# A two-layer encoder trunk on one core: seven-product tiles woven with plain tiles, and five groups of hidden values turned by VectorE

## The chip, the core and the metric

The kernel runs on one NeuronCore of one Trainium2 chip. A core has five engines that run their own instruction streams and wait for each other through semaphores: TensorE (PE; matrix products, into eight PSUM banks), VectorE (DVE), ScalarE (ACT), GpSimd (POOL) and SyncE (SP, which here only issues DMA transfers). The metric is the device time of one execution in microseconds (us); for the kernel before it is 938.8 us, the median of three runs (938.33 to 939.52).

## The reference

256 tokens of width 1024 go through two layers. A layer is a half-step SwiGLU feed-forward block, a mixing block (a windowed attention and a differential attention side by side) and a second feed-forward block. The change lies in the feed-forward blocks alone, of which there are four, called FFN 1 to FFN 4 here:

```python
D_MODEL, SEQ, DEPTH, D_FF = 1024, 256, 2, 2816

def swiglu(h, w_gate, w_up, w_down):
    return (jax.nn.silu(h @ w_gate) * (h @ w_up)) @ w_down

for l in range(DEPTH):
    x = x + 0.5 * swiglu(rms_norm(x, ffn1_norm[l]), ffn1_w_gate[l], ffn1_w_up[l], ffn1_w_down[l])
    ...
    x = x + 0.5 * swiglu(rms_norm(x, ffn2_norm[l]), ffn2_w_gate[l], ffn2_w_up[l], ffn2_w_down[l])
return rms_norm(x, final_norm)
```

All is float32.

## The kernel before

**Weight tiles.** A feed-forward block reads its weights in tiles of 512 rows by 512 columns (1 MB), in an order fixed in a list (`specs`, filled in `ffn_specs`, L244 to L261). A tile is loaded into one of six `raw` buffers by a DMA that SP issues (`emit_dma`, L148). Then it is split for the float32 product into a high part, rounded by ScalarE (a cast), and a remainder, subtracted by VectorE (`emit_split`, L176), in two halves of two row blocks each. The split halves lie in 14 `w` buffers, so seven halves, three and a half tiles, can stand ready. A product of two split operands takes three matmuls (high by high, remainder by high, high by remainder).

`weights()` (L233) is called where TensorE's instructions for the next tile are written. It first emits the splits that lie six halves ahead and the loads that fit into the raw buffers (`ahead`, L212), and the second half of a tile is emitted ahead in the same way when TensorE's instructions reach it. During the feed-forward blocks TensorE, VectorE, ScalarE and GpSimd execute their instructions in the order in which the program writes them (`Kept`, L41); each waits at its own instruction until what it needs is there. SP's DMAs are ordered by the scheduler of the framework, and executed in that order.

**Groups.** The 2816 hidden columns are five groups of 512 and a last one of 256. For a *plain* group, `tokens` (L496) multiplies the 256 tokens (two row blocks) by two gate tiles and two up tiles, 24 matmuls a tile, each into two PSUM banks; `gate` and `hidden` form Silu(gate) times up (ScalarE, then one VectorE "up" operation per row block).

Groups 2 and 4 (`SEVEN`) are done by seven products instead of eight. Tokens in two halves and input columns in two halves make four quarters of the operand; the tile's gate and up rows in two halves make four weight blocks: a (gate, first rows), b (up, first rows), c (up, last rows), d (gate, last rows). The seven products, 12 matmuls each (`prod`, L590), use sums and differences of the quarters (made once per block by `make_sums`, L333) and the weights a, b + c, d, c, a + b, a + b + c and a + b + c + d. Two of the sums, b into a and c into b, are made by DMAs that GpSimd issues and that add onto the raw buffer; the other two by VectorE, in pairs of adds on raw buffers. `by_seven` (L600) issues the products one after the other, with one of the two down tiles of the group before after the fourth and the other at the end, and combines them with seven VectorE operations of 128x512 and two "up" operations.

**Turning.** The hidden values have tokens on partitions, and the down product needs hidden columns there. Two ways are in the kernel. `turn` (L636) does it on TensorE: 8 transposes of 128x128 into two banks, then split by ScalarE and VectorE from PSUM. A `Flip` (L648) does it without TensorE: VectorE transposes 32x32 blocks, one instruction for each of the two row blocks; then eight DMAs of 64 KB, issued by SP, carry the block rows to their partitions; and `operands` (L658) lets ScalarE and VectorE split the result from SBUF. Before, `made` (L670) uses a Flip for groups 0 and 2 (`FLIP`), except in FFN 1, where `aside` is `attention_constants`. So groups 0 to 4 of FFN 1 and groups 1, 3 and 4 of the other three blocks are turned on TensorE: 14 turns. The last group of 256 columns is always turned there.

**Order of a block.** Group n's first tile, the turn of group n - 1, the rest of group n, then the two down tiles of group n - 1 (`down`, L678), which add into four PSUM banks kept through the block (L676). Four banks are left for everything else. After the last group's two tiles, `ffn_end` (L730) multiplies by group 4's down tiles. In FFN 1 and FFN 4 an `aside` is emitted ahead of group 3: the constants for attention (one TensorE transpose, VectorE and ScalarE operations), and the load of the final gain.

Of the kernel before, what the change touches and what calls it, by code (L numbers as in the profile page):

```python
# [18 lines left out]
FF = 2816  # L19
# [12 lines left out]
FLIP = (0, 2)  # L32
# [3 lines left out]
def trunk(ctx: ExitStack, tc: tile.TileContext, x, n1, g1, u1, d1, nm, w_in, sink,  # L36
# [79 lines left out]
    def seven(wg, wu, c0, downs):  # L116

        a, b, c, d = [object() for _ in range(4)]  # L120
        w = {a: rows(wg, c0, 512, 0, 4), b: rows(wu, c0, 512, 0, 4), c: rows(wu, c0, 512, 4, 4), d: rows(wg, c0, 512, 4, 4)}

        def load(k):
            return lambda t: [(t, w[k])]

        def gather(k, to):
            def add():
                pool.dma_start(raws[to], w[k], accum_op=ALU.add)
            return add

        def plus(x, to):
            def prep():
                for h in (0, 2):
                    x_, t_ = [raws[i][:, h:h + 2] for i in (x, to)]
                    dve.tensor_tensor(t_, t_, x_, op=ALU.add)
            return prep

        return [Step(4, 512, load(a), key=a, free=[]),
                Step(4, 512, load(b), key=b, behind=gather(c, b), prep=gather(b, a)),
                Step(4, 512, load(d), key=d, free=[]),  # L140
                Step(4, 512, load(c), key=c, free=[]),
                downs[0],
                Step(4, 512, None, src=a, free=[]),
                Step(4, 512, None, prep=plus(c, a), src=a, free=[c]),
                Step(4, 512, None, prep=plus(d, a), src=a, free=[a, d]),
                downs[1]]

# [95 lines left out]
    for l in range(DEPTH):  # L243
        def ffn_specs(wg, wu, wd):  # L244
            down = lambda g, h: plain(wd[l], h * 512, 512, 4 * g, 4)
            for k0 in (0, 4):
                specs.extend(plain(w[l], 0, 512, k0, 4) for w in (wg, wu))
            for g in range(1, NGRP):
                downs = [down(g - 1, h) for h in range(2)]
                if g in SEVEN:  # L250
                    specs.extend(seven(wg[l], wu[l], g * 512, downs))
                else:
                    specs.extend(plain(w[l], g * 512, 512, k0, 4) for w in (wg, wu) for k0 in (0, 4))
                    specs.extend(downs)
            for k0 in (0, 4):
                def gu_moves(t, k0=k0, ws=(wg[l], wu[l])):
                    return [(t[:, :, h * 256:h * 256 + 256], rows(w, FF - 256, 256, k0, 4)) for h, w in enumerate(ws)]
                specs.append(Step(4, 512, gu_moves))
# [31 lines left out]
    class Norm:  # L290
# [42 lines left out]
        def make_sums(self):  # L333
# [5 lines left out]
            def make(x, y, op):  # L339
                v = tmp().rearrange("p a (c s) -> p (a c) s", c=2)  # L340
                dve.tensor_tensor(v, x, y, op=op)
# [9 lines left out]
            s2 = make(s1, t0, ALU.add)  # L351
            yield
            make(t1, t0, ALU.subtract)
            yield
            make(b0, s2, ALU.subtract)
# [212 lines left out]
    def ffn(norm, aside=None, before=None, final=False):  # L568
# [21 lines left out]
        def prod(xo, w):  # L590
            acc = bank()
            for k in range(4):
                hi, lo = w.part(k)
                xh, xl = xo(k)
                pe.matmul(acc, lhsT=xh, rhs=hi, start=k == 0, stop=False)
                pe.matmul(acc, lhsT=xl, rhs=hi, start=False, stop=False)
                pe.matmul(acc, lhsT=xh, rhs=lo, start=False, stop=k == 3)
            return acc

        def by_seven(h, g):  # L600


            flat = lambda: tmp().rearrange("p a n -> p (a n)")

            def put(o, x, y, op):
                dve.tensor_tensor(o, x, y, op=op)
                return o

            m1, m7 = flat(), flat()
            act.copy(m1, prod(norm.quarter(0, 0), weights()))  # L610
            hT = turned(h)
            act.copy(m7, prod(norm.summed(2), weights(held=True)))
            p2 = prod(norm.quarter(0, 1), weights())
            g0 = put(flat(), p2, m1, ALU.add)
            p3 = prod(norm.summed(3), weights())
            silu(g0, g0, 0)
            down(hT, g - 1, 0, weights())
            h = blk(F32)
            p5 = prod(norm.summed(0), weights())
            p6 = prod(norm.summed(1), weights())  # L620
            u2 = put(flat(), p6, m1, ALU.subtract)
            u3 = put(m7, m7, u2, ALU.add)
            p4 = prod(norm.quarter(1, 1), weights())
            g1 = put(m1, p4, u3, ALU.subtract)
            w = weights()
            silu(g1, g1, 1)
            put(u3, u3, p5, ALU.subtract)
            put(u2, u2, p5, ALU.subtract)
            put(u2, u2, p3, ALU.add)
            up(h, u2, g0, 0)  # L630
            up(h, u3, g1, 1)
            h = made(h, g)
            down(hT, g - 1, 1, w)
            return h
# [61 lines left out]
        h = made(hidden(g, us), 0)  # L696
        for n in range(1, NGRP):
            sums = norm.make_sums() if n + 1 == min(SEVEN, default=0) else iter(())
            if n == 3 and aside is not None:
                aside()  # L700
            if n in SEVEN:
                h = by_seven(h, n)
                continue
            gs = [bank(), bank()]
            tokens(gs, norm.xs, weights(), 0)
            hT = turned(h)
            tokens(gs, norm.xs, weights(), 4)
            g = gate(gs)
            next(sums, None)
            us = [bank(), bank()]  # L710
            for k0 in (0, 4):
                tokens(us, norm.xs, weights(), k0)
                next(sums, None)
            h = made(hidden(g, us), n)
            for hh in range(2):
                down(hT, n - 1, hh, weights())
                if hh == 0:
                    next(sums, None)

        gu = [bank(), bank()]  # L720
        tokens(gu, norm.xs, weights(), 0)
        hT = turned(h)
        tokens(gu, norm.xs, weights(), 4)
# [362 lines left out]
```

## Time and profile before

| | |
|---|---|
| median of three runs | 938.8 us |
| profiled execution | 938.07 us |
| its span, first to last instruction | 936.3 us |
| TensorE busy | 924.3 us |
| VectorE busy | 710.7 us |
| ScalarE busy | 551.6 us |
| DMA moved | 189.34 MB, mean 202 GB/s |

The profile is one execution. The span is what the engine times are shares of; the time of a run holds some 2 us more than the span. "PE" is TensorE, "DVE" VectorE, "ACT" ScalarE, "SPq" SyncE's issue of DMAs. In a row of operations the text "out<-in" gives the program's names of the tiles: `ps` is a PSUM bank, `w` a split weight, `raw` a loaded tile, `s` a block of activations or hidden values (also a Flip's), `tmp` an intermediate of 128x512, `ident` the identity of a transpose. `s<-s` is a Flip's transpose, its DMA, or the split behind it. "x24" is a count, and "[0.53 <-DVE s L51]" says that the engine had been idle for 0.53 us and what ended it. All engine instructions are issued through one helper and carry its line, L51, so rows are told apart by tiles.

### The profile page before, as it was taken

The numbers are of one execution on the slowest core, as the hardware profiler recorded it, in microseconds if no ns is written. First come the engines' busy times: TensorE is split into PE (matmuls) and PEld (weight loads), VectorE is DVE, ScalarE is ACT, GpSimd is POOL, SyncE is SP. The second block draws the span as 40 slices with busy tenths as digits, with TensorE's granted clock in tenths as the row PEclk, the third lists the DMA queues.
The fourth block names the chain that finished last, engine by engine and source line by source line (L and its number), as shares of the span: only waits on it lengthen the run. The fifth ranks groups of instructions, "written<-read, shape, count | busy, mean of one in ns | idle before, by whom it ended". The sixth has DMA issues, their size and how long they took to land.

```text
span 936.3 us, 12889 instructions
## 1 busy us (share of the span) xinstructions
PE 924.3 (99%) x4796; PEld 784.7 (84%) x4796; DVE 710.7 (76%) x1010; ACT 551.6 (59%) x869; POOL 41.5 (4%) x65
## 2 busy tenths in 40 slices
PE   8999999999999999999999999999999999999997
PEld 6788788899898888888888888888999888888886
DVE  6679869779856479689765896896796655895992
ACT  7856556467735467276473664565685483664562
POOL 0400000000000000000000001000000000000001
PEclk9999999999999999999999999999999999999999
DMA  9986958746424876978658588686642447588721
GB/s 339 346 225 210 289 131 289 208 176 153 136 75 135 248 199 204 261 211 310 197 178 232 151 302 240 188 299 181 185 147 90 135 163 215 150 303 238 213 91 45
DMA packets 113583, 189.34 MB, mean 202 GB/s; under 512 B 4207, under 2 KB 38065, under 8 KB 113521
## 3 DMA queue, kind: packets, MB, share of 16 engines
q1 hardware_dynamic: 103728, 170.42, 55.0%
q0 software_dynamic: 8704, 17.07, 10.7%
q10 hardware_dynamic: 1088, 1.05, 0.3%
q8 instruction: 37, 0.61, 0.3%
q14 instruction: 26, 0.20, 0.1%
HBM read 184.32 MB, written 1.05 MB: 198 GB/s over the span
## 4 chain that ended last, share of the span: by engine, by line
PE 94%; DVE 2%; ACT 1%; issue 1%; DMA 0%; POOLq 0%; ACTq 0%; POOL 0%; DVEq 0%
PE ps L51 94%; DVE w L51 1%; ACT w L51 1%; DMA xk<-in_x_dram 0%; DVE raw L51 0%; ACT s L51 0%; DVE tmp L51 0%; DVE s L51 0%; ACT tmp L51 0%; ACT L51 0%; DVE xk L51 0%; POOLq L1081 0%; ACTq L51 0%; POOL rf L51 0%; DVE rf L51 0%
## 5 line engine op out<-in xcount | busy, mean ns | idle before, releaser
L51 PE MATMUL ps<-w,s 128*128 128x512 f32 (+1 forms) x2994 | 690.4, 390 | 0.5 <-DVE tmp L51 0.5
L51 PEld LDWEIGHTS ps<-w,s 128*128 128x128 f32 x2994 | 557.4, 188 | 115.8 <-DVE tmp L51 1.5
L51 DVE TENSOR_TENSOR w<-raw,w 128x1024 fp32r<-128x1024 f32 (+1 forms) x416 | 435.0, 1087 | 87.9 <-ACT w L51 85.5
L51 ACT CAST w<-raw 128x1024 fp32r<-128x1024 f32 (+1 forms) x416 | 372.5, 943 | 150.8 <-PE ps L51 93.1
L51 PE MATMUL ps<-s,w 128*128 128x256 f32 x672 | 84.0, 285 | 0.0
L51 PEld LDWEIGHTS ps<-s,w 128*128 128x128 f32 x672 | 81.7, 192 | 1.1
L51 PE MATMUL ps<-w,q 128*128 128x512 f32 x288 | 68.7, 392 | 0.0
L51 PEld LDWEIGHTS ps<-w,q 128*128 128x128 f32 x288 | 53.5, 188 | 10.8
L51 ACT CAST s<-s 128x512 fp32r<-128x512 f32 x12 | 6.9, 619 | 69.6 <-DMA s<-s 55.1
L51 DVE TENSOR_TENSOR s<-s,s 128x512 fp32r<-128x512 f32 x12 | 7.8, 689 | 50.5 <-ACT s L51 50.5
L51 ACT ACTIVATE s<-ps,gcol 128x256 fp32r<-128x256 f32 (+1 forms) x80 | 31.3, 476 | 20.9 <-PE ps L51 20.9
L51 DVE TENSOR_TENSOR raw<-raw,raw 128x1024 f32<-128x1024 f32 x32 | 37.6, 1218 | 0.0
L51 POOL DMA_DIRECT2D raw<-in_ffn_w_up_dram x16 | 20.8, 1298 | 363.6 <-DVE w L51 156.8
L51 ACT ACTIVATE s<-s,negm 128x256 f32<-128x256 f32 x64 | 31.9, 500 | 6.6 <-DVE negm L51 6.6
L51 PE MATMUL ps<-ident,s 128*128 128x128 f32 x256 | 33.6, 273 | 0.8 <-DVE s L51 0.8
L51 PEld LDWEIGHTS ps<-ident,s 128*128 128x128 f32 x256 | 29.5, 141 | 5.1 <-ACT w L51 0.9
L51 ACT CAST s<-ps 128x512 fp32r<-128x512 f32 x36 | 19.6, 591 | 21.9 <-PE ps L51 21.9
L51 DVE TENSOR_TENSOR s<-ps,s 128x512 fp32r<-128x512 f32 x36 | 23.3, 685 | 10.8 <-ACT s L51 10.8
L51 DVE SCALAR_TENSOR_TENSOR s<-ps,gcol,s 128x256 fp32r<-128x256 f32 x48 | 20.3, 478 | 14.6 <-ACT s L51 14.5
L51 ACT ACTIVATE tmp<-tmp,r 128x512 f32<-128x512 f32 x16 | 11.6, 722 | 27.1 <-DVE tmp L51 27.1
L51 ACT CAST q<-tmp 128x512 fp32r<-128x512 f32 x20 | 12.4, 620 | 20.9 <-DVE tmp L51 20.9
L51 ACT ACTIVATE tmp<-ps,r 128x512 f32<-128x512 f32 (+1 forms) x32 | 19.1, 629 | 6.9 <-PE ps L51 6.8
(110 smaller groups left out, 456.5 us busy)
## 6 DMA issues: line engine op xcount, KB each, us to landing
raw<-in_ffn_w_down_dram SPq DMA_DIRECT2D x44, 1024.0 KB, 5.3
raw<-in_ffn_w_gate_dram SPq DMA_DIRECT2D x39, 1024.0 KB, 5.9
raw<-in_ffn_w_up_dram SPq DMA_DIRECT2D x39, 1024.0 KB, 5.2
raw<-in_ffn_w_up_dram POOLq DMA_DIRECT2D x16, 1024.0 KB, 9.7
raw<-in_w_in_dram SPq DMA_DIRECT2D x14, 1024.0 KB, 5.9
raw<-in_ffn_w_gate_dram SPq DMA_DIRECT2D x8, 512.0 KB, 4.5
raw<-in_ffn_w_up_dram SPq DMA_DIRECT2D x8, 512.0 KB, 5.5
raw<-in_w_in_dram SPq DMA_DIRECT2D x8, 512.0 KB, 5.1
```

The lines of the kernel that those rows point to most:

```text
L51: ins = issue(*a, **k)
```

## The change

The order of a feed-forward block, from group 1 on, is written out in one list (`ORDER`), from which both the loads and the instructions are made. Tiles of the seven-groups alternate with tiles of plain groups, down tiles and tiles of the last group. In the terms above, after group 0 the order of tiles is: plain 1, seven 2 a, plain 1, seven 2 d, two of plain 1, seven 2 c, down 0, seven 2 a+b, down 0, seven 2 a+b+c, plain 3, seven 2 b+c, plain 3, seven 2 a+b+c+d, two of plain 3, seven 4 a, down 1, seven 4 d, down 1, seven 4 c, down 2, seven 4 a+b, down 2, seven 4 a+b+c, last, seven 4 b+c, down 3, seven 4 a+b+c+d, last, down 3. Then come group 4's down tiles, as before.

Four of the seven products (a, a+b+c, b+c, a+b+c+d) add one after the other into one PSUM bank, which is read between them; one of the token sums changes its sign for it. The combining takes four VectorE operations and one more ScalarE operation than before. The weights a, d and c of a seven-group stay in their raw buffers until their sums are made.

Groups 0 to 4 are all turned by a Flip, in all four blocks; `turn` remains for the last 256 columns. The `aside` moves behind the last group's second tile, ahead of the second down tile of group 3. The sums of the operand are made from the start of group 1 on.

```diff
-FLIP = (0, 2)
+def order():
+    two, four = [[("seven", g, p) for p in ("a", "d", "c", "ab", "abc", "bc", "abcd")] for g in (2, 4)]
+    one, three = [[("plain", g, (w, k0)) for w in range(2) for k0 in (0, 4)] for g in (1, 3)]
+    downs = [[("down", g, h) for h in range(2)] for g in range(4)]
+    last = [("last", 0, k0) for k0 in (0, 4)]
+    sums = [("sums", 0, 1)]
+    turn = [[("turned", g, 0)] for g in range(4)]
+    aside = [("aside", 0, 0)]
...
+    seq = sums + one[:1] + sums + two[:1] + sums + one[1:2] + sums + two[1:2] + turn[0] + one[2:]
+    seq += two[2:3] + downs[0][:1] + two[3:4] + downs[0][1:]
+    seq += weave(two[4:], three) + turn[1]
+    seq += four[:1] + downs[1][:1] + four[1:2] + turn[2] + downs[1][1:] + four[2:3] + downs[2][:1] + four[3:4] + turn[3] + downs[2][1:] + four[4:5]
+    seq += last[:1] + four[5:6] + downs[3][:1] + four[6:] + last[1:] + aside + downs[3][1:]
+    return seq
...
+        def step(self, part):
+            k = self.key
+            return dict(
+                a=lambda: Step(4, 512, self.load("a"), key=k["a"], free=[]),
+                d=lambda: Step(4, 512, self.load("d"), key=k["d"], free=[]),
+                c=lambda: Step(4, 512, self.load("c"), key=k["c"], free=[]),
+                ab=lambda: Step(4, 512, None, src=k["a"], free=[]),
+                abc=lambda: Step(4, 512, None, prep=self.plus("c", "a"), src=k["a"], free=[k["c"]]),
+                bc=lambda: Step(4, 512, self.load("b"), key=k["b"], behind=self.gather("c", "b")),
+                abcd=lambda: Step(4, 512, None, prep=self.plus("d", "a"), src=k["a"], free=[k["a"], k["d"]]))[part]()
...
+        class Seven:
...
+            def a(self):
+                self.acc = prod(norm.quarter(0, 0))
+                self.m1 = self.flat()
+                act.copy(self.m1, self.acc)
+
+            def d(self):
+                g0 = self.put(prod(norm.quarter(0, 1)), self.m1, ALU.add, self.m1)
+                self.m1 = None
+                self.g0 = silu(g0, g0, 0)
+
+            def c(self):
+                self.z = self.flat()
+                act.copy(self.z, prod(norm.summed(3)))
+
+            def ab(self):
+                p5 = prod(norm.summed(0))
+                self.v = self.flat()
+                act.mul(self.v, p5, -1.0)
+                self.put(self.z, p5, ALU.subtract, self.z)
+
+            def abc(self):
+                prod(norm.summed(1), self.acc)
+                self.put(self.z, self.acc, ALU.subtract, self.z)
+                self.h = blk(F32)
+                up(self.h, self.z, self.g0, 0)
+                self.z = self.g0 = None
+
+            def bc(self):
+                prod(norm.summed(2), self.acc)
+                self.put(self.v, self.acc, ALU.subtract, self.v)
+
+            def abcd(self):
+                prod(norm.quarter(1, 1), self.acc)
+                g1 = silu(self.flat(), self.acc, 1)
+                up(self.h, self.v, g1, 1)
+                self.v = self.acc = None
+                hid[self.g] = Flip(self.h)
...
-        def made(h, g):
-            return Flip(h) if g in FLIP and aside is not attention_constants else h
-
-        def turned(h):
-            return h.operands() if isinstance(h, Flip) else turn(h, 2)
...
+        hid, hT, groups = {0: Flip(hidden(g, us))}, {}, {}
+        sums = norm.make_sums()
+        for what, n, part in ORDER:
...
+            elif what == "down":
+                down(hT[n], n, part, weights())
+                if part:
+                    del hT[n]
+            elif what == "turned":
+                hT[n] = hid.pop(n).operands()
...
+            elif what == "aside" and aside is not None:
                 aside()
...
-        hT = turned(h)
-        tokens(gu, norm.xs, weights(), 4)
+        hT = hid.pop(NGRP - 1).operands()
         h = hidden(gate([b[:, 0:256] for b in gu]), [b[:, 256:512] for b in gu])
         return accs, hT, lambda: turn(h, 1)
```

More of the change, by code (lines that the diff above doesn't have):

```diff
@@ L612, in by_seven @@
[L612 to L622, printed above, removed]
@@ L695, in ffn @@
         tokens(us, norm.xs, weights(), 4)
[L696 to L699, printed above, removed]
-                aside()
[L701 to L722, printed above, removed]
-        tokens(gu, norm.xs, weights(), 4)
+        hid, hT, groups = {0: Flip(hidden(g, us))}, {}, {}
+        sums = norm.make_sums()
+        for what, n, part in ORDER:
+            if what == "seven":
+                getattr(groups.setdefault(n, Seven(n)), part)()
+            elif what == "plain":
+                groups.setdefault(n, Plain(n)).part(*part)
+            elif what == "down":
+                down(hT[n], n, part, weights())
[3 more added lines that the diff above has]
+                hT[n] = hid.pop(n).operands()
+            elif what == "sums":
+                for _ in range(part):
+                    next(sums, None)
+            elif what == "aside" and aside is not None:
+                aside()
+            elif what == "last":
+                if part == 0:
+                    gu = [bank(), bank()]
+                tokens(gu, norm.xs, weights(), part)
+        hT = hid.pop(NGRP - 1).operands()
         h = hidden(gate([b[:, 0:256] for b in gu]), [b[:, 256:512] for b in gu])
```

121 lines of the change are left out of this document (66 added, 55 removed).

## The prediction, made before the result was known

> **What bounds the kernel now.** I read the engine shares first, then the chain that ended last, then a table of one undisturbed stretch (the second feed-forward block, FFN 2), then TensorE's timeline around a turn.
>
> The page's busy shares, and its chain by engine:
>
> ```profile
> PE 924.3 (99%) x4796; PEld 784.7 (84%) x4796; DVE 710.7 (76%) x1010; ACT 551.6 (59%) x869; POOL 41.5 (4%) x65
> ...
> PE 94%; DVE 2%; ACT 1%; issue 1%; DMA 0%; POOLq 0%; ACTq 0%; POOL 0%; DVEq 0%
> ```
>
> The table by stretch (start:end, length, then busy time and instructions of each engine, granted clock, DMA share, GB/s):
>
> ```profile
> 305.00:480.00 175.00, 175.00 (x795) 145.11 (x794) 135.17 (x148) 99.49 (x129) 5.86 (x5) 1.00 0.75 228
> ```
>
> TensorE is busy for all of these 175 us at full clock, while VectorE (third figure) has 40 us to spare and ScalarE 75. So inside a block an instruction taken off TensorE shortens the program by its whole length, and work put on VectorE, ScalarE or a queue costs nothing until TensorE waits for it.
>
> TensorE's timeline in FFN 1: three stretches with a turn in each:
>
> ```profile
> 29.67 6.28 PE L51 MATMUL ps<-w,s 128*128 128x512 f32 x27
> 36.48 0.30 PE L51 MATMUL ps<-ident,s 128*128 128x128 f32 x1 [0.53 <-DVE s L51]
> 37.05 0.98 PE L51 MATMUL ps<-ident,s 128*128 128x128 f32 x7 [0.26 <-DVE s L51]
> 37.79 30.19 PE L51 MATMUL ps<-w,s 128*128 128x512 f32 x132
> 67.81 1.03 PE L51 MATMUL ps<-ident,s 128*128 128x128 f32 x8
> 68.61 2.99 PE L51 MATMUL ps<-w,q 128*128 128x512 f32 x12
> ...
> 94.78 1.29 PE L51 MATMUL ps<-w,s 128*128 128x512 f32 x5
> 96.01 0.25 PE L51 MATMUL ps<-ident,grow 34*128 34x34 f32 x1
> 96.18 0.96 PE L51 MATMUL ps<-w,s 128*128 128x512 f32 x3
> 97.65 5.06 PE L51 MATMUL ps<-w,s 128*128 128x512 f32 x21 [0.50 <-DVE tmp L51]
> ```
>
> Matmuls overlap, so starts are compared, not durations. 132 matmuls from 37.79 to 67.81 are 0.227 us each; a tile of 24 is therefore 5.45 us, a product of 12 is 2.73. A turn, 8 transposes, is 68.61 - 67.81 = 0.80 us. The first turn costs more: 27 matmuls from 29.67 end at 35.80, and the next matmul starts at 37.79, so 1.99 us, as VectorE is late with the hidden values.
>
> **The change part by part.**
>
> *Turns off TensorE.* Turned on TensorE before: groups 0 to 4 in FFN 1, and 1, 3, 4 in FFN 2 to 4, 14 in all; none afterwards. 13 x 0.80 + 1.99 = 12.4 us off the path. This is the whole gain; matmuls are neither added nor removed.
>
> *What VectorE and ScalarE get.* Rows by group and shape (count | busy us, mean ns):
>
> ```profile
> L51 DVE TENSOR_TENSOR w<-raw,w 128x1024 fp32r<-128x1024 f32 x312 | 367.9, 1221 | 71.6 <-ACT w L51 69.6
> L51 ACT CAST w<-raw 128x1024 fp32r<-128x1024 f32 x312 | 313.6, 1052 | 120.3 <-PE ps L51 71.6 <-DVE raw L51 42.2 <-DMA raw<-in_ffn_w_up_dram 2.8
> L51 DVE TENSOR_TENSOR tmp<-ps,tmp 128x512 f32<-128x512 f32 x24 | 16.4, 683 | 0.0
> L51 DVE STREAM_TRANSPOSE s<-s 128x512 f32<-128x512 f32 x12 | 12.3, 1060 | 0.0
> L51 DVE SCALAR_TENSOR_TENSOR s<-ps,hr,tmp 128x512 f32<-128x512 f32 x24 | 16.9, 745 | 0.0
> L51 ACT ACTIVATE tmp<-ps,r 128x512 f32<-128x512 f32 x24 | 15.2, 681 | 1.4 <-PE ps L51 1.4
> L51 DVE TENSOR_TENSOR s<-s,s 128x512 fp32r<-128x512 f32 x12 | 7.8, 689 | 50.5 <-ACT s L51 50.5
> L51 ACT CAST s<-s 128x512 fp32r<-128x512 f32 x12 | 6.9, 619 | 69.6 <-DMA s<-s 55.1 <-DMA s<-in_final_norm_dram 14.5
> L51 ACT COPY tmp<-ps 128x512 f32<-128x512 f32 x16 | 9.4, 586 | 8.2 <-PE ps L51 8.2
> ```
>
> 14 Flips of two transposes at 12.3/12 = 1.03 us are +28.7 us of VectorE. Seven combining adds become four in each of 8 seven-groups: 24 x 0.68 = -16.4 us. The splits behind a turn keep their count. ScalarE gets one evacuation more per seven-group, 8 x 0.59 = 4.7. VectorE comes to about 723 of 930 us, 78%: hidden.
>
> *The weave.* It matters where VectorE's work is dense. A split weight tile is two halves, 2 x 367.9/312 = 2.36 us; a pair of raw adds is about as long. In the old run of a seven-group VectorE has 9 tiles (21.2), two pairs (4.7), seven adds (4.8), two "up" and a Flip (3.6): 34 us against 7 x 2.73 + 2 x 5.45 = 30.0 of TensorE. In the new order the densest run, from the third part of group 2 to its fifth (5 tiles, TensorE 19.1 us), has 11.8 of splits, 4.7 of pairs, 2.1 for two adds and an "up", 3.4 of group 1's "up" and Flip: 22 us, 3 us late. The split runs 3 tiles ahead, at least 2.73 + 5.45 + 2.73 = 10.9 us, so TensorE does not see it. Cost 0; if the lead is gone, 3 us in each block. Nothing here can be gained in FFN 2, whose TensorE is already full.
>
> *One bank for four products.* The product that adds onto the bank must wait for VectorE's read of the sum before. Between them always lies a tile of 24 matmuls, 5.45 us, against 0.68 us of reading and a VectorE up to 3 us late: 0. A plain group beside it finds two of the eight banks fewer, and its "up" half must wait until the gate banks are read: two Silu at 0.68 us against one product, 2.73: 0, with about 1 us to spare.
>
> *The Flip's queue work.* Each Flip issues 8 DMAs on SP. The first two of FFN 2, with what POOL issued beside them and when ScalarE got the data:
>
> ```profile
> 316.83 8.57 SPq L656 DMA_DIRECT2D s<-s  x8
> 384.02 3.14 SPq L656 DMA_DIRECT2D s<-s  x5
> 384.02 8.10 SPq L656 DMA_DIRECT2D s<-s  x8
> ...
> 315.57 1.32 POOL L51 DMA_DIRECT2D raw<-in_ffn_w_up_dram  x1 [9.21 <-DVE s L51]
> 385.18 1.28 POOL L51 DMA_DIRECT2D raw<-in_ffn_w_up_dram  x1 [41.86 <-DVE s L51]
> ...
> 328.05 1.15 ACT L51 CAST s<-s 128x512 fp32r<-128x512 f32 x2 [9.86 <-DMA s<-s]
> 395.87 1.14 ACT L51 CAST s<-s 128x512 fp32r<-128x512 f32 x2 [13.77 <-DMA s<-s]
> ```
>
> First issue to first use is 11.2 and 11.9 us, and both ran into an adding load of POOL. Before that load bites, five issues take 3.14 us, 0.63 each. 112 more DMAs hold SP for up to 14 x 8.6 = 120 us, and the weight loads behind them wait up to 8.6 us each time. Six raw buffers and three split tiles lie ahead of TensorE; where three raw buffers are pinned by a seven-group, three are left, with about 11 us between a buffer's release and the use of its next load. Cost 0, with little to spare.
>
> Groups 0 to 3 have 16.4, more than 30, 21.8 and 27.3 us of other TensorE work between their last matmul and their turn: hidden. **Group 4 has two tiles, 48 x 0.227 = 10.9 us**, and nothing follows them on TensorE but its own down product. Its path after the last matmul: 0.2 to ScalarE (that matmul's tail), Silu 0.68, "up" 0.75, first transpose 1.03, which makes 2.7; eight issues at 0.63, 5.0; from the last issue to ScalarE 328.05 - 325.40 = 2.65; cast 0.62, subtraction 0.69 and 0.1 of handing over. Sum 11.8, needed at 10.9 + 0.23 (the second matmul reads the remainder): 0.7 us of stall. No POOL load is due there, as group 4's second one follows a load issued some 20 us earlier, so I take the quick issue. Bounds: 0, and with issues as slow as 8.57 and a landing of 3.75 us (395.87 - 392.12) 5.4 us. For FFN 2 to 4: 3 x 0.7 = 2.1.
>
> In FFN 1 the attention constants are emitted into exactly that gap:
>
> ```profile
> 100.81 0.19 DVE L51 COPY gcol<-ps 128x34 f32<-128x34 f32 x1
> 103.17 0.41 DVE L51 TENSOR_REDUCE lsum<-s 128x4 f32<-128x256 f32 x1
> 103.61 0.20 ACT L51 ACTIVATE lex<-lsum 128x4 f32<-128x4 f32 x1 [5.34 <-DVE lsum L51]
> ```
>
> These six VectorE operations take 2.8 us and ScalarE waits for their end. Counted from the start of the second-last tile: VectorE is through the Flip and two splits at 6.2, through the constants at 9.0; ScalarE then does the exponential, the two casts that stand behind it (to 11.5) and the turned values; VectorE its five small operations and two splits, to 13.9, then the remainder, to 14.6. Needed at 11.1: 3.5 us. Where the constants stand now TensorE loses 1.0 (94.78 to 97.65 for 8 matmuls of 1.82), which goes.
>
> *Sum.* -12.4 - 1.0 + 3.5 + 2.1 = -7.8 us. Against the profiled run (938.07, span 936.3) 930.3; the median of the three runs is 0.7 higher, so **931**.
>
> The Trainium skill speaks against the edit: "VectorE: DVE Perf Modes", section "The three transpose paths", advises TensorE for a 128x128 transpose whose result may lie in PSUM, at 390 ns. By that figure 112 transposes would free 44 us, an estimate; the trace has 0.10 us each in a row, and it decides. [...]
>
> **The rivals.**
>
> *A, slower: group 4's Flip is as late as today's Flips.* Then all four blocks stall for 5 us: -13.4 + 20 = +7, 946. For it: every measured Flip took 11 to 12 us. Against: each had a POOL load beside it. It turns slower once the stall exceeds 3.4 us a block. A stall this long may also slow the clock: at the program's start 20 matmuls took 6.17 us,
>
> ```profile
> 6.19 6.17 PE L51 MATMUL ps<-w,s 128*128 128x512 f32 x20
> ```
>
> where 4.7 is normal, so 1.5 us more per stall, 952. (The Trainium skill, "TensorE: Matmul & The Clock Gate", part 1, states that an idle window of about 3.4 us halves the clock; the page shows full clock up to its last slice, so no run here shows it yet.)
>
> *B, the weave is late.* Three pinned raw buffers, a bank read late, or SP behind its Flips stall TensorE about 1 us per seven-group: 8 us, 939, no change. For it: VectorE is 3 us late at one place. Against: the old order is denser and FFN 2 shows no idle TensorE.
>
> *C, all hidden.* Group 4's Flip and the constants cost nothing: -13.4, 925.
>
> **How the numbers follow.** Forecast 0.60 (its own range 927 to 935), A 0.17, B 0.13, C 0.10. Low is 925, C's time; high 944, which cuts off most of A: about 0.15 left out above and 0.04 below. A change within 0.2% (1.9 us) cannot be told from none here. Faster: forecast, C and a little of B, 0.72; same 0.06; slower 0.22.
>
> **What would show it.** TensorE's busy time falls by about 12 us and its transposes by 112. In FFN 2, 3 and 4 TensorE idles about 0.7 us just before the first matmul of group 4's down product, ended by VectorE's subtraction; in FFN 1 about 3.5. The Flips of group 4 take 5 to 6 us to issue, those beside POOL's loads 8 or more. Elsewhere in the blocks TensorE does not idle. It is wrong if idle time comes in the woven tiles (B), or if the last Flip's issue takes 8 us (A).

## The result, and the profile after

The changed kernel takes 944.1 us (median of five runs, 941.13 to 946.82) against 938.5 for the kernel before: ratio 1.0058, 95% interval 1.0033 to 1.0083. It is slower by 0.6%; the forecast was 931 and faster. The profiled execution is the shortest of the five: 941.13 us, span 939.4, that is 3.1 us over the profiled execution of before.

From the page of the changed kernel, its engine shares, the chain by engine and two groups of TensorE (busy us, mean ns | idle before, releaser). The helper's line is L77 now, the Flip's DMAs are L728, the weight loads L180:

```profile
PE 916.9 (98%) x4684; PEld 774.1 (82%) x4684; DVE 725.5 (77%) x1014; ACT 564.2 (60%) x877; POOL 42.6 (5%) x65
...
PE 85%; DVE 6%; issue 3%; DMA 2%; ACT 2%; SPq 0%; ACTq 0%; DVEq 0%; POOLq 0%; POOL 0%
...
L77 PE MATMUL ps<-w,s 128*128 128x512 f32 (+1 forms) x2994 | 692.8, 390 | 3.9 <-DVE s L77 3.1
...
L77 PE MATMUL ps<-w,q 128*128 128x512 f32 x288 | 71.2, 397 | 7.7 <-DVE tmp L77 7.7
```

The 112 transposes are gone, but TensorE's part of the chain falls from 94% to 85%. The group `ps<-w,q` now has 7.7 us of idle time ended by VectorE's `tmp`: TensorE waits for the shared bank to be read. `ps<-w,s` has 3.1 us ended by VectorE's `s`: turned hidden values come late.

**The bank.** TensorE, then VectorE, ScalarE, SP and GpSimd in FFN 2 around product b+c of group 2 (timeline: start, us, engine; in brackets the idle time before):

```profile
362.25 2.88 PE L77 MATMUL ps<-w,q 128*128 128x512 f32 x12
364.96 5.60 PE L77 MATMUL ps<-w,s 128*128 128x512 f32 x24
371.34 3.00 PE L77 MATMUL ps<-w,q 128*128 128x512 f32 x12 [0.77 <-DVE tmp L77]
...
360.80 0.68 DVE L77 TENSOR_TENSOR tmp<-tmp,ps 128x512 f32<-128x512 f32 x1
362.89 2.36 DVE L77 TENSOR_TENSOR w<-raw,w 128x1024 fp32r<-128x1024 f32 x2 [1.41 <-ACT w L77]
365.96 2.36 DVE L77 TENSOR_TENSOR w<-raw,w 128x1024 fp32r<-128x1024 f32 x2 [0.71 <-ACT w L77]
368.24 2.35 DVE L77 TENSOR_TENSOR raw<-raw,raw 128x1024 f32<-128x1024 f32 x2
370.51 0.68 DVE L77 TENSOR_TENSOR tmp<-tmp,ps 128x512 f32<-128x512 f32 x1
...
361.80 2.01 ACT L77 CAST w<-raw 128x1024 fp32r<-128x1024 f32 x2 [2.06 <-DMA raw<-in_ffn_w_up_dram]
364.88 2.00 ACT L77 CAST w<-raw 128x1024 fp32r<-128x1024 f32 x2 [1.07 <-DMA raw<-in_ffn_w_gate_dram]
...
350.77 7.61 SPq L728 DMA_DIRECT2D s<-s  x8
358.48 1.28 SPq L180 DMA_DIRECT2D raw<-in_ffn_w_gate_dram  x1
...
352.30 1.28 POOL L77 DMA_DIRECT2D raw<-in_ffn_w_up_dram  x1 [36.52 <-DVE s L77]
```

Product a+b+c (362.25) is done at 365.1. VectorE reads its bank at 370.51, 5.4 us later, because the read stands in VectorE's queue behind a split and the pair of raw adds for a later tile, 4.7 us of work whose results are not yet needed, and behind two waits for ScalarE (1.41 and 0.71). ScalarE in turn waited for the adding load (issued 352.30, used 361.80) and for a gate tile whose load SP issued only after the Flip's eight DMAs (358.48). Product b+c is ready at 370.4 and starts at 371.34: 0.93 us, counted from start to start less 0.227. In FFN 3 and FFN 4 the same wait is 1.24 and 1.28 us. In FFN 1 it is 4.90, TensorE's rows and VectorE's:

```profile
78.47 5.60 PE L77 MATMUL ps<-w,s 128*128 128x512 f32 x24
88.81 4.57 PE L77 MATMUL ps<-w,q 128*128 128x512 f32 x12 [4.74 <-DVE tmp L77]
...
87.98 0.68 DVE L77 TENSOR_TENSOR tmp<-tmp,ps 128x512 f32<-128x512 f32 x1
```

It is the same queue, some 4 us later against TensorE than in FFN 2. VectorE brings that lateness from the start of the block. Its "up" operations of group 0 in FFN 1 and in FFN 2:

```profile
36.06 1.40 DVE L77 SCALAR_TENSOR_TENSOR s<-ps,hr,tmp 128x512 f32<-128x512 f32 x2
...
318.66 1.40 DVE L77 SCALAR_TENSOR_TENSOR s<-ps,hr,tmp 128x512 f32<-128x512 f32 x2
```

TensorE's last matmul of group 0 is over at about 31.0 us in FFN 1 and at 318.65 in FFN 2 (72 matmuls of 0.227 us from 14.64 and from 302.29). So VectorE is at once there in FFN 2 and 5 us late in FFN 1, and it does not catch up before the bank.

The twelve matmuls behind the wait take 4.4 us from start to start instead of 2.73. The stretches say why, and give FFN 2 to its last two tiles (granted clock is the third figure from the end):

```profile
83.00:89.00 6.00, 1.26 (x6) 0.78 (x5) 5.53 (x6) 3.21 (x4) 0.00 (x0) 0.98 1.05 387
89.00:92.00 3.00, 3.00 (x8) 2.32 (x9) 3.00 (x4) 1.80 (x3) 0.00 (x0) 0.50 1.05 388
305.00:460.00 155.00, 153.33 (x673) 125.78 (x672) 127.40 (x131) 94.89 (x114) 5.86 (x5) 1.00 0.81 243
```

The clock is halved after the wait, which costs 1.7 us more (4.40 - 2.73). FFN 2, without an idle moment before, now has 1.7 us.

**Group 1's turn.** FFN 2 before down 1, TensorE, then VectorE:

```profile
389.82 6.51 PE L77 MATMUL ps<-w,s 128*128 128x512 f32 x28
396.80 7.57 PE L77 MATMUL ps<-w,s 128*128 128x512 f32 x32 [0.47 <-DVE s L77]
...
392.74 1.43 DVE L77 SCALAR_TENSOR_TENSOR s<-ps,hr,tmp 128x512 f32<-128x512 f32 x2
394.09 2.08 DVE L77 STREAM_TRANSPOSE s<-s 128x512 f32<-128x512 f32 x2
396.09 1.25 DVE L77 TENSOR_TENSOR s<-s,s 128x512 fp32r<-128x512 f32 x2
```

Group 1's turned values had long arrived. Their subtraction (396.09) stands behind group 3's "up" and transposes, which wait for group 3's last matmul; one product later TensorE needs them. 0.63 us in each of the four blocks.

**Group 4's turn.** FFN 2: SP, ScalarE and TensorE; then TensorE in FFN 1:

```profile
448.43 5.94 SPq L728 DMA_DIRECT2D s<-s  x8
...
456.25 1.14 ACT L77 CAST s<-s 128x512 fp32r<-128x512 f32 x2 [1.39 <-DMA s<-s]
...
456.92 0.50 PE L77 MATMUL ps<-w,s 128*128 128x512 f32 x1 [0.20 <-ACT s L77]
457.65 3.70 PE L77 MATMUL ps<-w,s 128*128 128x512 f32 x15 [0.23 <-DVE s L77]
...
177.56 4.17 PE L77 MATMUL ps<-w,s 128*128 128x512 f32 x17 [1.04 <-DVE s L77]
```

0.86 us in FFN 2, none in FFN 3 and 4, 1.3 in FFN 1.

**The sum, start to start, for the two profiled runs.** Turns off TensorE -12.4, the constants' old wait -1.0; waits for the bank 4.90 + 0.93 + 1.24 + 1.28 = +8.4 and the half clock +1.7; group 1's turn 4 x 0.63 = +2.5; before down 0 of FFN 1 (61 us) +0.9, of which 0.2 is group 0's turned values and 0.7 a split weight behind them in VectorE's queue; group 4's turn 1.3 + 0.86 = +2.2; the program's start, where nothing was changed, +0.7 (the matmuls behind the first 24 begin at 14.64 us instead of 13.91). Together +3.0 against 3.1 measured. The median is 3 us above this profiled run. The five runs' mean granted clocks are 0.996 (941.1 and 942.8 us), 0.994 (944.1) and 0.993 (945.4 and 946.8), so longer runs spent more time at half clock; where, no trace of this kernel shows.

### The profile page after: what moved, and what is told of

Its sections match the earlier page's. It is cut to its first block, busy times and chain, and to the rows that moved or that the text cites. A ratio compares the mean times of both kernels' runs of the same rounds, so it can differ in the third digit from the quotient of the medians.

```text
span 939.4 us, 12905 instructions
## 1 busy us (share of the span) xinstructions
PE 916.9 (98%) x4684; PEld 774.1 (82%) x4684; DVE 725.5 (77%) x1014; ACT 564.2 (60%) x877; POOL 42.6 (5%) x65
## 4 chain that ended last, share of the span: by engine, by line
PE 85%; DVE 6%; issue 3%; DMA 2%; ACT 2%; SPq 0%; ACTq 0%; DVEq 0%; POOLq 0%; POOL 0%
PE ps L77 85%; DVE w L77 2%; DVE s L77 2%; ACT w L77 2%; DVE raw L77 1%; DMA raw<-in_ffn_w_gate_dram 1%; DVE tmp L77 1%; DMA xk<-in_x_dram 0%; SPq L728 0%; DMA s<-s 0%; ACT tmp L77 0%; ACT s L77 0%; ACT L77 0%; ACTq L77 0%; DVEq L77 0%
## 5 line engine op out<-in xcount | busy, mean ns | idle before, releaser
L77 PE MATMUL ps<-w,s 128*128 128x512 f32 (+1 forms) x2994 | 692.8, 390 | 3.9 <-DVE s L77 3.1
L77 PEld LDWEIGHTS ps<-w,s 128*128 128x128 f32 x2994 | 558.0, 188 | 122.3 <-DVE s L77 6.2
L77 DVE TENSOR_TENSOR w<-raw,w 128x1024 fp32r<-128x1024 f32 (+1 forms) x416 | 436.9, 1087 | 121.1 <-ACT w L77 117.4
L77 ACT CAST w<-raw 128x1024 fp32r<-128x1024 f32 (+1 forms) x416 | 379.0, 943 | 221.9 <-PE ps L77 146.1
L77 PE MATMUL ps<-s,w 128*128 128x256 f32 x672 | 84.0, 285 | 0.0
L77 PEld LDWEIGHTS ps<-s,w 128*128 128x128 f32 x672 | 81.7, 192 | 1.1
L77 PE MATMUL ps<-w,q 128*128 128x512 f32 x288 | 71.2, 397 | 7.7 <-DVE tmp L77 7.7
L77 PEld LDWEIGHTS ps<-w,q 128*128 128x128 f32 x288 | 54.9, 192 | 20.7 <-ACT w L77 9.3
L77 ACT ACTIVATE s<-ps,gcol 128x256 fp32r<-128x256 f32 (+1 forms) x80 | 31.4, 478 | 21.0 <-PE ps L77 21.0
L77 DVE STREAM_TRANSPOSE s<-s 128x512 f32<-128x512 f32 x40 | 41.3, 1069 | 0.0
L77 POOL DMA_DIRECT2D raw<-in_ffn_w_up_dram x16 | 20.8, 1298 | 378.6 <-DVE s L77 137.2
L77 DVE TENSOR_TENSOR raw<-raw,raw 128x1024 f32<-128x1024 f32 x32 | 37.6, 1217 | 0.0
L77 ACT ACTIVATE s<-s,negm 128x256 f32<-128x256 f32 x64 | 31.8, 500 | 6.5 <-DVE negm L77 6.5
L77 ACT CAST q<-tmp 128x512 fp32r<-128x512 f32 x20 | 12.4, 620 | 38.7 <-DVE tmp L77 38.7
L77 DVE TENSOR_TENSOR s<-s,s 128x512 fp32r<-128x512 f32 x40 | 25.7, 683 | 11.2 <-ACT s L77 11.2
L77 DVE SCALAR_TENSOR_TENSOR s<-ps,gcol,s 128x256 fp32r<-128x256 f32 x48 | 20.3, 478 | 14.8 <-ACT s L77 14.7
L77 ACT ACTIVATE tmp<-ps,r 128x512 f32<-128x512 f32 (+1 forms) x40 | 24.5, 642 | 7.5 <-PE ps L77 6.8
L77 ACT CAST s<-s 128x512 fp32r<-128x512 f32 x40 | 22.6, 615 | 1.9 <-DMA s<-s 1.9
L77 PE MATMUL ps<-w,v 128*128 128x512 f32 x96 | 23.1, 389 | 0.0
L77 PEld LDWEIGHTS ps<-w,v 128*128 128x128 f32 x96 | 18.0, 188 | 3.7
L77 DVE SCALAR_TENSOR_TENSOR s<-ps,hr,tmp 128x512 f32<-128x512 f32 (+1 forms) x32 | 20.5, 679 | 0.2 <-ACT tmp L77 0.2
L77 DVE TENSOR_TENSOR q<-tmp,q 128x512 fp32r<-128x512 f32 x20 | 13.8, 689 | 8.3 <-ACT q L77 8.3
```

The costliest lines, as they stand in the source:

```text
L77: ins = issue(*a, **k)
```

## The experiments

All ratios are against the kernel before, with 95% intervals; diffs are against the changed kernel unless they say otherwise.

### The read of the shared bank ahead of the next split

```diff
             def abc(self):
-                prod(norm.summed(1), self.acc)
+                prod(norm.summed(1), self.acc, weights(1, True))
```

`prod` takes the tile as an argument; splits are emitted one half less far ahead and not in the product's middle, so the read of a+b+c comes before them in VectorE's queue.

> Only VectorE's queue is reordered: in both seven-groups the read of the shared bank behind product a+b+c now stands ahead of the split of the tile two further on and ahead of the pair of raw adds. Theory (the read stands behind late work in VectorE's queue, and TensorE's next product onto the bank waits for it): the idle times of 4.9, 0.9, 1.2 and 1.3 us before product b+c of group 2 go, and with them the half-clock stretch of FFN 1 (1.9 us): about 10 us less than the changed kernel, 931 to 935. Rival (VectorE simply has too much to do in this stretch, the read is only where it shows): the idle time moves to the next tiles, at most 2 us gained, 940 to 943.

Measured: 936.0 us (933.27 to 936.83), ratio 0.9969 [0.9957, 0.9981], 1 us above the theory's range. FFN 2, TensorE and VectorE:

```profile
366.37 2.88 PE L77 MATMUL ps<-w,q 128*128 128x512 f32 x12
...
358.38 2.36 DVE L77 TENSOR_TENSOR w<-raw,w 128x1024 fp32r<-128x1024 f32 x2 [0.93 <-ACT w L77]
361.13 0.69 DVE L77 TENSOR_TENSOR tmp<-tmp,ps 128x512 f32<-128x512 f32 x1 [0.40 <-PE ps L77]
...
362.52 2.35 DVE L77 TENSOR_TENSOR w<-raw,w 128x1024 fp32r<-128x1024 f32 x2
```

The read now waits 0.40 us for TensorE instead of the reverse, the split follows it, and no product b+c waits in any block. The adding load is nearly as late as before (issued 348.21, used 357.30, 9.1 us). Same work, same banks, same loads: what cost 8 us was the place of one 0.7 us instruction. In FFN 1 the next product onto the bank, a+b+c+d, now waits 2.1 us: part of VectorE's arrears is left there, and it is why the range was missed.

### Group 1's turn ahead of group 3's last two products

```diff
-    seq += weave(two[4:], three) + turn[1]
+    seq += weave(two[4:], three[:2]) + turn[1] + three[2:]
```

> Group 1's turn is emitted ahead of the last two tiles of group 3, not behind them. Theory (group 1's data had long landed, its split only stood behind group 3's Flip on VectorE, with one product of cover): the four gaps of 0.6 us before group 1's first down tile go, 2.5 to 3 us less than the changed kernel, about 941; the stall at b+c stays. Rival (the data of the Flip itself is late): ScalarE waits for the Flip's DMAs at the new place, and the time is that of the changed kernel, 944, or more.

Measured: 941.0 us (939.76 to 944.16), ratio 1.0028 [1.0017, 1.0039]: 3 us below the changed kernel. FFN 2, TensorE and VectorE:

```profile
384.82 20.56 PE L77 MATMUL ps<-w,s 128*128 128x512 f32 x90
...
388.01 1.26 DVE L77 TENSOR_TENSOR s<-s,s 128x512 fp32r<-128x512 f32 x2
```

Ninety matmuls without a gap; the four waits of 0.63 us are gone, those for the bank stay (6.7, 0.9, 1.0, 1.3). In FFN 2 to 4 the two losses are separate. In FFN 1 the wait is longer in this profile, and half clock lasts 6.8 us there instead of 3.4; the mean clock is 0.994, as in the median run of the changed kernel, which may have lost its time there too.

### Banks of their own

```diff
-                prod(norm.summed(2), self.acc)
-                self.put(self.v, self.acc, ALU.subtract, self.v)
+                self.put(self.v, prod(norm.summed(2)), ALU.subtract, self.v)
...
-                prod(norm.quarter(1, 1), self.acc)
-                g1 = silu(self.flat(), self.acc, 1)
+                g1 = silu(self.flat(), prod(norm.quarter(1, 1)), 1)
```

The sum over all four products is left out.

> Products b+c and a+b+c+d get a bank of their own, so TensorE need not wait for the read of the bank before. Left out: these two products are no longer added onto those before. Theory (shared bank): the idle time before b+c goes in all four blocks, 931 to 935, as with the read put first. Rival (VectorE or a weight tile is late anyway): TensorE waits as long at the next weight tile, 940 to 944.

Measured: 931.9 us (931.40 to 932.58), ratio 0.9927 [0.9913, 0.9942]. No product b+c waits for a bank. Left are group 1's turn (0.6 us in FFN 2 to 4, 1.55 in FFN 1), group 4's turn, and in FFN 1 1.1 us before down 0 and 0.77 before plain group 3's third tile, where it waits for VectorE's read of a bank. So sharing the bank, with the reads where they stood, cost 12 us of the 944.

### Group 1 turned on TensorE

```diff
-                    hid[self.g] = Flip(hidden(self.gate, self.acc))
+                    h = hidden(self.gate, self.acc)
+                    hid[self.g] = h if self.g == 1 else Flip(h)
...
-                hT[n] = hid.pop(n).operands()
+                h = hid.pop(n)
+                hT[n] = h.operands() if isinstance(h, Flip) else turn(h, 2)
```

It takes away the Flip that holds SP just before the late loads.

> Group 1 is turned on TensorE, so its Flip's 8 DMAs no longer hold SP for 7 us and VectorE has 2 us less before the stall. Four turns of 0.8 us come back. If SP's hold makes the load of group 3's second gate tile late: that load is issued some 7 us earlier, the stall before b+c goes in FFN 2 to 4 and falls to 2 or 3 us in FFN 1, below the length that halves the clock: 4.9 + 1.9 + 3.4 - 2.5 less and 3.2 more, plus the 2.5 us of late split of group 1, together about 937 to 940. If the raw buffers pinned by the seven-group make it late: the load is issued no earlier, and the time is 943 to 946.

Measured: 957.1 us (955.15 to 961.22), ratio 1.0201 [1.0173, 1.0229], far above both ranges. The waits for the bank grew to 7.3, 4.1, 3.5 and 3.2 us, with a half clock behind all but the 3.5 of FFN 3. FFN 2: SP, GpSimd, ScalarE, TensorE:

```profile
355.26 0.37 SPq L180 DMA_DIRECT2D raw<-in_ffn_w_gate_dram  x1
357.53 5.06 SPq L180 DMA_DIRECT2D raw<-in_ffn_w_up_dram  x2
...
355.44 1.28 POOL L77 DMA_DIRECT2D raw<-in_ffn_w_up_dram  x1 [36.43 <-DVE w L77]
...
369.01 3.90 ACT L77 CAST w<-raw 128x1024 fp32r<-128x1024 f32 x4 [7.95 <-DMA raw<-in_ffn_w_up_dram]
...
377.74 2.62 PE L77 MATMUL ps<-w,q 128*128 128x512 f32 x7 [3.94 <-DVE tmp L77]
```

The theory that SP's hold made the tile b+c late falls: with SP free, 3 MB of plain loads go out beside GpSimd's adding load, and its data are used 13.6 us after its issue (355.44 to 369.01) instead of 9.5 (352.30 to 361.80). ScalarE stands at that cast for 8 us, and everything behind it in VectorE's queue, the read of the bank too.

### Without the adding load of c

```diff
-                bc=lambda: Step(4, 512, self.load("b"), key=k["b"], behind=self.gather("c", "b")),
+                bc=lambda: Step(4, 512, self.load("b"), key=k["b"]),
```

Product b+c is then of b alone. First with VectorE turning all groups:

> Left out: the weight block c is not added into b, so that product runs with b alone; one adding load of two is gone in each seven-group. If the lateness of that adding load is what delays VectorE's queue: ScalarE's wait of 2 us for the tile goes, and with it the stalls of about 1 us before b+c in FFN 2 to 4; in FFN 1 at most 3 us of 4.9 remain, without half clock: 933 to 938. If VectorE's own work and queue order make the stall, it stays: 940 to 945.

Measured: 934.5 us (933.04 to 935.26), ratio 0.9953 [0.9940, 0.9967]. The waits for the bank go in FFN 2 to 4; 2.6 us stay in FFN 1. Then with group 1 turned on TensorE:

> Group 1 turned by TensorE as in the earlier run (957.1 us), and c is not added into b by a DMA (left out, so product b+c is of b alone). There the adding load took 13.5 us in FFN 2 and the stalls before product b+c were 7.3, 4.1, 3.5 and 3.2 us. If the slowed adding load made that kernel worse, the stalls go and the kernel costs 4 turns of .80 over the one without the gather and with VectorE's turn (934.5): 937 to 941 us. If something else (TensorE's turn of group 1 itself, or the copies out of the banks on VectorE) did it: 950 us or more.

Measured: 931.7 us (931.35 to 932.70), ratio 0.9928 [0.9915, 0.9942]. The group `ps<-w,q`, which had 17.4 us of idle time with group 1 on TensorE and the adding load in place:

```profile
L77 PE MATMUL ps<-w,q 128*128 128x512 f32 x288 | 69.3, 389 | 0.5 <-DVE tmp L77 0.5
```

So the adding load made that kernel worse: between the two lie 25 us. It came out 5 us below the range: I had added four turns of 0.80 and forgotten what goes with VectorE's turn, 4 x 0.63 us and 1.9 of the 2.6 of FFN 1. These make 4.5 of the 6.0 us by which it lies below 934.5 + 3.2. That the plain loads beside it slow the adding load is only read from the rows of two kernels; no run moved the loads alone.

### The two halves of the change, each alone

The new order with the old choice of turns (groups 0 and 2 by VectorE, outside FFN 1):

```diff
+        def made(h, g):
+            return Flip(h) if g in (0, 2) and aside is not attention_constants else h
+        def turned(h):
+            return h.operands() if isinstance(h, Flip) else turn(h, 2)
```

> The weave and the shared bank stay; turning is as in the kernel before (Flips for groups 0 and 2 in FFN 2 to 4, all else on TensorE), so the order alone is judged. If the order is harmless and the Flips cost the time, this is near the kernel before, 937 to 941. If, as the run with group 1 on TensorE suggests, the late tile b+c is what TensorE waits for and weight loads that are not held back by a Flip slow the adding load further, the stall before b+c is 3 to 7 us in each block, and with the transposes back on TensorE it is 955 to 965.

Measured: 964.0 us (963.46 to 965.00), ratio 1.0267 [1.0251, 1.0283]. The waits for the bank are 5.4, 4.4, 2.9 and 3.2 us, each with a half clock.

The old order with the new turns, from the kernel before:

```diff
-FLIP = (0, 2)
+FLIP = (0, 1, 2, 3, 4)
...
-            return Flip(h) if g in FLIP and aside is not attention_constants else h
+            return Flip(h) if g in FLIP else h
```

> The kernel before, with Flips for groups 0 to 4 in all blocks and nothing else: no weave, no shared bank. TensorE gets its 12.4 us off. If a Flip is hidden in the old order too, 926 to 929, and the weave was not needed. If ScalarE, which must wait 11 to 12 us for the Flip's data with a tile or less of other work of TensorE in between, eats up the lead of the splits, stalls of 2 to 5 us come behind groups 1, 3 and 4 in each block: 940 to 955.

Measured: 971.0 us (969.03 to 972.76), ratio 1.0343 [1.0325, 1.0361], above both ranges. FFN 2, group 4's turn, TensorE and SP:

```profile
457.67 10.54 PE L51 MATMUL ps<-w,s 128*128 128x512 f32 x45 [1.19 <-DVE tmp L51]
471.45 4.93 PE L51 MATMUL ps<-w,s 128*128 128x512 f32 x10 [3.24 <-ACT s L51]
...
463.14 5.74 SPq L656 DMA_DIRECT2D s<-s  x8
```

Here the turned values are waited for 3.4 us, at a quick issue, and the clock halves: ten matmuls take 4.9 us. Other waits of 0.7 to 3.0 us stand in every block. Each half alone costs 25 to 32 us, both together 6. The order gives VectorE's turns their cover. That the Flip before the late loads keeps them off the adding load is argued from the run with group 1 on TensorE, not shown by itself.

### All moves at once

The read first and the turn early as above; group 1's sums of tokens spread over its four tiles; the `aside` two products earlier.

```diff
-    seq = sums + one[:1] + sums + two[:1] + sums + one[1:2] + sums + two[1:2] + turn[0] + one[2:]
+    seq = sums + one[:1] + sums + two[:1] + one[1:2] + sums + two[1:2] + turn[0] + one[2:3] + sums + one[3:]
...
-    seq += four[:1] + downs[1][:1] + four[1:2] + turn[2] + downs[1][1:] + four[2:3] + downs[2][:1] + four[3:4] + turn[3] + downs[2][1:] + four[4:5]
-    seq += last[:1] + four[5:6] + downs[3][:1] + four[6:] + last[1:] + aside + downs[3][1:]
+    seq += four[:1] + downs[1][:1] + four[1:2] + turn[2] + downs[1][1:] + four[2:3] + downs[2][:1] + four[3:4] + turn[3] + downs[2][1:] + aside + four[4:5]
+    seq += last[:1] + four[5:6] + downs[3][:1] + four[6:] + last[1:] + downs[3][1:]
```

> The changed kernel with four things moved: the read of the shared bank first, group 1's turn ahead of group 3's last two tiles, the four token sums spread over group 1's four tiles, the aside two products earlier. Theory: gone are the stalls before b+c, the four gaps of 0.6 us, and 1.3 us at the end of FFN 1; the sums shorten VectorE's lag in FFN 1. 925 to 931. Rival (the late tile b+c is the cause, queue order only a part): 2 to 5 us remain in FFN 1, 931 to 935.

Measured: 935.5 us (933.37 to 938.01), ratio 0.9967 [0.9957, 0.9977], above the theory's range. FFN 2 to 4 idle only at group 4's turn, 1.1 us at most. FFN 1 is worse:

```profile
62.35 1.95 PE L77 MATMUL ps<-w,v 128*128 128x512 f32 x3 [4.30 <-ACT v L77]
...
62.33 0.69 DVE L77 TENSOR_TENSOR v<-tmp,v 128x512 fp32r<-128x512 f32 x1 [0.68 <-ACT v L77]
```

Product c waits for the last sum of tokens, made too late, for 4.5 us, and 2.0 us go at group 4's turn, both with a half clock behind. So spreading the sums was a bad move. The turn waited 1.3 us in the changed kernel, so the earlier `aside` seems bad too; it was not moved alone.

### The sums earlier instead, and then both reads first

From the changed kernel: the read first, the turn early, the first sum made in group 0, the `aside` ahead of product d of group 4:

```diff
-    seq = sums + one[:1] + sums + two[:1] + sums + one[1:2] + sums + two[1:2] + turn[0] + one[2:]
+    seq = one[:1] + sums + two[:1] + sums + one[1:2] + sums + two[1:2] + turn[0] + one[2:]
...
-    seq += four[:1] + downs[1][:1] + four[1:2] + turn[2] + downs[1][1:] + four[2:3] + downs[2][:1] + four[3:4] + turn[3] + downs[2][1:] + four[4:5]
-    seq += last[:1] + four[5:6] + downs[3][:1] + four[6:] + last[1:] + aside + downs[3][1:]
+    seq += four[:1] + downs[1][:1] + aside + four[1:2] + turn[2] + downs[1][1:] + four[2:3] + downs[2][:1] + four[3:4] + turn[3] + downs[2][1:] + four[4:5]
+    seq += last[:1] + four[5:6] + downs[3][:1] + four[6:] + last[1:] + downs[3][1:]
...
         g = gate(gs)
+        sums = norm.make_sums()
+        next(sums)
         tokens(us, norm.xs, weights(), 4)
...
-        sums = norm.make_sums()
```

> The changed kernel with four moves of place: VectorE's read of the shared bank ahead of the split for the next group, group 1's turn ahead of group 3's last two products, group 2's work beside group 4 two products earlier but behind the table load's place, and the first of FFN 1's token sums made in group 0. Theory (the losses are places in VectorE's queue): the stalls before products b+c and a+b+c+d (4.9, .9, 1.2, 1.3 us and the half clock of 1.9) and the .6 us before down 1 in each block all go, nothing takes their place: 928 to 932 us. Rival (VectorE's lag in FFN 1, from its sums and splits taking turns with ScalarE, is a debt that moves with every order): 2 to 5 us of stalls stay in FFN 1 and the time is 932 to 936, no better than the read first alone at 936.0.

Measured: 929.2 us (928.59 to 931.82), ratio 0.9909 [0.9896, 0.9923]. One wait of 1.7 us for the bank stays in FFN 1, before a+b+c+d. The next run puts the read of b+c first as well:

```diff
             def bc(self):
-                prod(norm.summed(2), self.acc)
+                prod(norm.summed(2), self.acc, weights(1, True))
```

> The fastest kernel so far (929.2 us) with VectorE's read of product b+c too put ahead of the split for the next tiles. What is left there in FFN 1 is a wait of 1.71 us before product a+b+c+d, whose bank VectorE reads at 92.30 behind four halves of splits (87.75, 4.63 us). If that wait is again only the place of the read in VectorE's queue: it goes, and the time is 927 to 928.5. Rival (VectorE is behind with the splits themselves by then, so the product would wait for its own weights instead): the wait changes its releaser and the time stays at 929 to 930.

Measured: **926.5 us** (925.69 to 929.47), ratio 0.9868 [0.9852, 0.9884], just below the theory's range. The page's group that had 7.7 us of idle time:

```profile
L77 PE MATMUL ps<-w,q 128*128 128x512 f32 x288 | 69.2, 389 | 0.0
```

And FFN 2 by stretch, 0.4 us idle instead of 1.7:

```profile
305.00:460.00 155.00, 154.58 (x683) 127.48 (x682) 128.33 (x130) 91.54 (x106) 5.17 (x4) 1.00 0.81 247
```

The same instructions in another order beat the kernel before by 12 us, close to the 13.4 that the turns and the constants' old wait were worth. What is left in the profiled run, the longest of the four, is group 4's turn: 1.4 us in FFN 1, 0.9 and 1.1 in FFN 2 and 3.

## Why the prediction was wrong

*Turns off TensorE* (-12.4) held: the last kernel above shows that the time is there to be had. *What VectorE and ScalarE get* held: VectorE 725.5 us against 723 forecast.

*The step that failed is "One bank for four products"*, at 0. I compared 5.45 us of cover with 0.68 of reading and a VectorE "up to 3 us late". The lateness was sized from the sum of VectorE's work. What counts is the time at which one instruction's turn comes in a queue that runs in written order: ahead of the read stood 4.7 us of split and raw adds for later tiles, and VectorE's own waits for ScalarE, which waits for loads. The read came 5.4 us after the product in FFN 2, some 9 us after it in FFN 1 (78.6 to 87.98). Price: 8.4 us, 1.7 of half clock, and by the run with separate banks 12 us of the median. The error fits rival B in kind (a bank read late), but B priced it at about 1 us for each seven-group. The eight seven-groups gave 0.9 to 1.3 in three group 2s, 4.9 in one, none in group 4. The 4.9 had its sign in the prediction's own rows: the first turn of FFN 1 cost 1.99 us because VectorE was late there, and only its removal was counted. The same lateness then fell on the bank.

*"The weave"*, also at 0, held for the weights but for 0.7 us before down 0 of FFN 1: the product b+c waited for its bank, not for its tile. But the 3 us there was taken as the whole lateness, without the waits for ScalarE and the loads.

*"The Flip's queue work"*, 0 "with little to spare": the adding load beside a Flip (used at 361.80) and the plain load behind it (364.88) were late for ScalarE, which fed the lost place above. But its sign was not what I thought: without that Flip the adding load is later still, and 957 us came out.

*"Groups 0 to 3 … hidden"*: wrong for group 1. I counted TensorE's work ahead of the turn, more than 30 us, and not what stands ahead of the turn's subtraction on VectorE: 4 x 0.63 us. For group 0 in FFN 1 it was 0.2, and 0.7 for the split behind it.

*Group 4's Flip* had the right mechanism: issues took 5.94 us (5.0 assumed), and the wait was 0.86 in FFN 2 but none in FFN 3 and 4, so 0.9 for 2.1. *The constants in FFN 1* were over-sized: 3.5 forecast, 1.3 measured. Rival A did not occur, but the half clock that I had noted under it did, behind another wait. The Trainium skill, "TensorE: Matmul & The Clock Gate", part 1, states half rate after an idle window of about 3.4 us; the row 89.00:92.00 at 0.50, behind 4.9 us without matmuls, agrees. But the 20 slow matmuls at the program's start, from which I had priced it, were no sign of it: the granted clock of the kernel before is 1.00 from 6 to 12 us. What slowed them is not shown. The price came out near all the same, 1.7 us for 1.5, by luck.

## What to carry to other kernels

Where an accumulator is shared, look up what stands ahead of its read in the reader's queue, instruction by instruction, with that engine's own waits; neither the reader's busy share nor the sum of its work tells when the read comes. Put such reads, and the last step of a hand-over, ahead of prefetch work that nobody needs yet. And try the parts of a change together: here each half alone was far worse than both, and five changes of place turned 6 us of loss into 12 of gain.

## What was not expected of the hardware

**Half clock came behind a wait of 2.9 us and not behind one of 3.5.** The new order with old turns, FFN 3: TensorE's timeline and two stretches:

```profile
563.83 4.57 PE L77 MATMUL ps<-w,q 128*128 128x512 f32 x12 [2.70 <-DVE tmp L77]
...
561.04:564.45 3.41, 0.71 (x4) 0.57 (x4) 3.37 (x5) 2.31 (x3) 0.00 (x0) 1.00 1.04 398
564.45:567.86 3.41, 3.41 (x10) 2.63 (x9) 3.41 (x5) 1.78 (x2) 0.00 (x0) 0.50 1.05 392
```

Group 1 on TensorE, FFN 3, the same:

```profile
561.00 3.00 PE L77 MATMUL ps<-w,q 128*128 128x512 f32 x12 [3.30 <-DVE tmp L77]
...
556.07:559.48 3.41, 1.62 (x8) 1.00 (x6) 3.41 (x4) 0.36 (x2) 0.00 (x0) 1.00 0.75 247
559.48:562.90 3.42, 1.90 (x8) 1.61 (x9) 3.38 (x5) 3.21 (x4) 0.00 (x0) 1.00 1.05 399
```

After 2.9 us of waiting, counted from start to start, the clock fell 0.6 us into the next matmuls and was back 3.4 us later. After 3.5 us it stayed at 1.00 (561.00 to 567.80). After 2.6 (without the adding load, FFN 1) it did not fall either. Waits of 4.5 and 2.0 us (all moves at once) were followed by half clock, waits of 2.1 and 1.7 were not. So length alone does not decide.

The times at which the clock fell show what else does. In each run with several falls they lie whole multiples of 3.413 us apart: in the new order with old turns at 86.59, 376.72, 564.45 and 851.17 us, which are 85, 140 and 224 such steps after the first; in the changed kernel 248 steps lie between its two. Inside the blocks half clock lasts 3.41 or 6.83 us, one step or two. The wait of 2.9 us lay almost whole in one step, in which TensorE was busy for 0.71 us of 3.41; the wait of 3.5 us was shared by two. Over all runs, from 20 to 925 us, every step at full clock with TensorE idle for more than 55% of it was followed by half clock, and none with 45% or less; between the two both happened. The page of the Trainium skill named above calls its window free-running, which agrees.

**An adding load took longer beside plain loads**: 9.5 us from issue to use with SP held by a Flip, 13.6 with three plain loads of 1 MB issued beside it. These are the rows of two kernels; no run shows the cause.
